# A fp32 decoder trunk on one core: weight combinations of the first FFN tiles on VectorE, and the last operand sets made between the first tile's products

## The chip, the core and the metric

The kernel runs on one core of a Trainium2 chip. A core has TensorE (matmuls, whose sums stand in PSUM), VectorE, ScalarE and GpSimd for work on tiles in SBUF, and SyncE, whose queue issues most of the DMAs. Every engine takes its own instructions in order and waits for the others by semaphores. The metric is the device time of one execution in microseconds; less is better. Names in the profile: PE is TensorE, PEld its weight loads, DVE VectorE, ACT ScalarE, POOL GpSimd, SP SyncE.

## What is computed

The program is a trunk of two layers over 1024 positions of width 1024, in float32. Each layer has a mixer (convolution and gMLP in layer 0, latent attention and mLSTM in layer 1), then a SwiGLU FFN, then a gated embedding. The change lies in the FFN alone, which both layers run:

```python
D_FF = -(-8 * D_MODEL // (3 * 256)) * 256        # 2816

def swiglu(h, w_gate, w_up, w_down):
    return (jax.nn.silu(h @ w_gate) * (h @ w_up)) @ w_down
...
    h = h + swiglu(rmsnorm(h, g_ffn[layer]), w_gate[layer], w_up[layer], w_down[layer])
```

## The kernel before

**Products.** Every fp32 matmul is done as three in a rounded format: each operand x is split into a high part (ScalarE casts it, L146) and a low part x - high (VectorE subtracts, L147), and `mm3` (L189 to L191) issues high x high, high x low and low x high into one PSUM accumulator. A tile is 128 x 512; one split therefore costs one ScalarE and one VectorE instruction.

**The way up.** `h @ w_gate` and `h @ w_up` use a scheme of seven block products in place of eight (Strassen's, in Winograd's form). The activations are cut in four by width and by position, the weights in four by row half and by column half. A unit of work is a pair of output tiles, i and i + 11, for the gate or for the up matrix, so there are 11 gate and 11 up units. Each takes seven products of 12 matmuls, numbered 1 to 7; product k multiplies the k-th combination of weights (made by `w_chain`, L167, and split by `w_halves`) by the k-th set of right operands `XC[k]`, four split tiles (`xch`, `xcl` in the profile). Sets 1 and 2 are made while the mixer ends. Sets 6, 7, 5, 4 and 3 are made by the generator `second_half` of `mixer_out`, in nine steps: four that normalize, subtract and make set 6, two for set 7, and one each for sets 5, 4 and 3. In the profile `h`, `t` are these activations, and L421 and L461 their normalization and subtractions.

**Weights.** `supply` is a second generator, moved on by one step at the end of every product (`prod`). It first loads the weight quarters of products 1 and 2, and then, unit by unit, the four quarters for the rest, forms four combinations of them (L179 to L181 and L510: `sg`, `su` are sums, `rg`, `ru` the loaded quarters of gate and up) and splits them (`hg`, `lg`, `hu`, `lu`). Loaded quarters and combinations share six buffers of tag `raw`. In this version all combinations are made on GpSimd.

**Order of the first units.** `ahead` are the gate and up units of pairs 0 and 1, `third` those of pair 2. Since sets 6 to 3 aren't ready yet, all six units first do products 1 and 2. Product 1's accumulator is copied out (`p1`, L580) and product 2 is then added on top of it in PSUM; the sum of both, after silu for the gate (`out11`, L548) or multiplied by it for the up unit (L551), frees the accumulator. The program holds six such accumulators (`ps`), all taken by these six units. Then `p6` and `rest` do products 6, 7, 5, 4, 3 of each unit in turn: two accumulators `pa`, `pb` are used again for products 4 and 3, after VectorE has read them (L593, L533). For an up unit GpSimd then multiplies by the gate and forms combinations for the way down (L540, L561), which are stored; the next pair's gate writes into the buffers that these stores read. The framework places the instructions of each engine in an order of its own at build time, by dependencies and priorities, so an engine's order isn't that of the code line by line. Where the words "first tile" stand, unit 0 of `ahead` is meant.

Of the kernel before, what the change touches and what calls it, by code (L numbers as in the profile page):

```python
# [16 lines left out]
ALU = mybir.AluOpType  # L17
# [29 lines left out]
class Build:  # L47
# [28 lines left out]
    def name(self, s):  # L76
        self.uid += 1
        return f"{s}_{self.uid}"
# [87 lines left out]
        self.split(hi, lo, t)  # L166
        return [(hi[:, k, :], lo[:, k, :]) for k in range(4)]  # L167

    def w_chain(self, w, c0, c1, name):


        tt = self.nc.gpsimd.tensor_tensor
        raw = lambda: self.wp.tile([P, 4, P], F32, tag="raw", name=self.name(f"s{name}"), bufs=RAW)
        a11 = self.w_quarter(w, 0, c0, name)
        a21 = self.w_quarter(w, 0, c1, name)
        a22 = self.w_quarter(w, 1, c1, name)
        a12 = self.w_quarter(w, 1, c0, name)
        s1, s2 = raw(), raw()
        tt(out=s1, in0=a21, in1=a22, op=ALU.add)  # L179
        tt(out=s2, in0=s1, in1=a11, op=ALU.subtract)  # L180
        tt(out=a21, in0=a11, in1=a21, op=ALU.subtract)  # L181
        return {1: a11, 2: a12, 4: a22, 5: s1, 6: s2, 7: a21}
# [142 lines left out]
def trunk(ctx, tc, x, p, positions, g_mix, g_ffn, g_ple, ev_w_in, ev_w_conv, ev_g_v, ev_w_s,  # L325
          ev_b_s, ev_w_out, od_w_in, od_b_gate, od_g_qa, od_g_kva, od_w_q_up, od_w_kv_up, od_g_q,
          od_g_k, od_g_mh, od_w_out, w_gate, w_up, w_down, w_ple_proj, w_ple_gate, out):
    nc = tc.nc
    B = Build(tc)
    x = x[0]  # L330
    out = out[0]
# [152 lines left out]
    def ffn_up(l, XC, second_half, act_d, down):  # L484

        half = NFF // 2
        sg, act = {}, {}
        c2 = lambda i: slice(i * P, (i + 1) * P)
# [4 lines left out]
        def supply():  # L493


            name = lambda d: "gu"[d["up"]]
            for part in (ahead, third):
                for k in (1, 2):
                    for d in part:
                        t = B.w_quarter(d["w"], k - 1, c2(d["i"]), name(d))  # L500
                        d["u"][k] = B.w_halves(t, name(d))
                        yield
            for d in ahead + third + later:
                i = d["i"]
                r = B.w_chain(d["w"], c2(i), c2(i + half), name(d))
                for k in (6, 7, 5, 4, 3) if i < 3 else (1, 6, 2, 7, 5, 4, 3):
                    d["u"][k] = B.w_halves(r[k], name(d))
                    if k == (6 if i < 3 else 2):
                        r[3] = r[2]
                        nc.gpsimd.tensor_tensor(out=r[3], in0=r[2], in1=r[6], op=ALU.subtract)  # L510
                    yield
            for s in range(AHEAD):
                down(s)
                yield

        def prod(d, k, ps=None):

            begins = ps is None
            ps = B.ps(f"p{k}") if begins else ps
            B.part_mm(ps, d["u"].pop(k), XC[k], begins)  # L520
            next(weights, None)
            return ps

        def spot(d, key):
            j = int(key[0]) * 2 - 3 + int(key[1])
            if not d["up"]:
                return B.slot(56 + d["i"] % 2 * 4 + j, F32, "sg")
            return B.slot(68 if j == 0 and d["i"] % 2 else 64 + j, F32, "act")

        def out(d, key, a, b):  # L530

            t = spot(d, key)
            nc.vector.tensor_tensor(out=t, in0=a, in1=b, op=ALU.add)  # L533
            if not d["up"]:
                nc.scalar.activation(t, t, AF.Silu)
                sg[d["i"], key] = t
                return
            act[d["i"], key] = t
            last = d["i"] == half - 1
            (nc.vector if last else nc.gpsimd).tensor_tensor(  # L540
                out=t, in0=t, in1=sg[d["i"], key], op=ALU.mult
            )
            operands(d["i"], key)

        def out11(d, t):

            if not d["up"]:
                nc.scalar.activation(t, d["X"], AF.Silu)  # L548
                sg[d["i"], "11"] = t
            else:  # L550
                nc.vector.tensor_tensor(out=t, in0=d["X"], in1=sg[d["i"], "11"], op=ALU.mult)  # L551
                act[d["i"], "11"] = t
# [33 lines left out]
            u2 = d["p1"]  # L586
            nc.vector.tensor_tensor(out=u2, in0=prod(d, 6), in1=u2, op=ALU.add)

        def rest(d):
            u2 = d["p1"]  # L590
            pa = prod(d, 7)
            u3 = B.tmp("u3")
            nc.vector.tensor_tensor(out=u3, in0=pa, in1=u2, op=ALU.add)  # L593
            pb = prod(d, 5)
            out(d, "22", pb, u3)
            prod(d, 4, pa)
            out(d, "21", pa, u2)
            prod(d, 3, pb)
            out(d, "12", pb, u2)


        more = second_half()
        ahead = [start(i, up) for i in range(2) for up in range(2)]
        third = [start(2, up) for up in range(2)]
        later = [start(i, up) for i in range(3, half) for up in range(2)]
        early = [dp.tile([P, HT], F32, name=B.name("early")) for _ in range(3)]
# [6 lines left out]
                next(more)  # L613
        for j, d in enumerate(ahead):
            p2(d)
            if j in (1, 2):
                next(more)
        for d, t in zip(third, early):
            p1(d, B.tmp("p1"))
            nc.sync.dma_start(t, d["p1"])  # L620
            next(more)
        for d in third:
            p2(d)
            out11(d, B.tmp("o11"))
            next(more)
        nc.sync.dma_start(early[2], act[2, "11"])
        for _ in more:
            pass
        for d in ahead:
            out11(d, spot(d, "11"))  # L630
        for d in ahead:
            p6(d)
            rest(d)
        for d, t in zip(third, early):
            d["p1"] = load(t, "p1")
            p6(d)
            if d["up"]:
                t = act[2, "11"] = spot(d, "11")
# [9 lines left out]
    half = NFF // 2  # L648
# [304 lines left out]
    for hq in range(2):  # L953
        t = B.tp.tile([P, 4, P], F32, tag="S", name=B.name("wsr"), bufs=2)
        nc.sync.dma_start(t, ev_w_s[0, hq * 4 : hq * 4 + 4].rearrange("h t s -> t h s"))
        nc.gpsimd.affine_select(
            out=t, in_=t, pattern=[[0, 4], [-1, P]], compare_op=ALU.is_ge, fill=0.0, base=0,
# [82 lines left out]
    for ch in range(4):  # L1040
# [13 lines left out]
        for n in range(2):  # L1054
# [6 lines left out]
            w = [col(CONV + i * 4 + ch) for i in range(3)]  # L1061
            nc.scalar.activation(y, z[n][:, 2:], AF.Copy, scale=w[2])
            for i in (1, 0):
                nc.vector.scalar_tensor_tensor(
                    out=y, in0=z[n][:, i : i + HT], scalar=w[i], in1=y, op0=ALU.mult, op1=ALU.add
# [127 lines left out]
    for i in range(16):  # L1193
# [3 lines left out]
        out=ang, in0=posf.unsqueeze(2).to_broadcast([P, NT, 16]),  # L1197
        in1=freq.unsqueeze(1).to_broadcast([P, NT, 16]), op=ALU.mult,
# [3 lines left out]
        out=turns, in0=ang, scalar1=1.0 / (2 * math.pi), scalar2=ROUND, op0=ALU.mult, op1=ALU.add  # L1202
    )
    nc.vector.tensor_scalar(
        out=turns, in0=turns, scalar1=-ROUND, scalar2=None, op0=ALU.add
    )
    fl = lambda t: t.rearrange("p a b -> p (a b)")
    for c in (TWO_PI_A, TWO_PI_B, TWO_PI_C):
        nc.vector.scalar_tensor_tensor(
            out=fl(ang), in0=fl(turns), scalar=-c, in1=fl(ang), op0=ALU.mult, op1=ALU.add  # L1210
        )
    nc.vector.tensor_scalar(
        out=ang, in0=ang, scalar1=3.1415925, scalar2=-3.1415925, op0=ALU.min, op1=ALU.max
# [5 lines left out]
        out=fl(ang), in0=fl(ang), scalar=-1.0, in1=fl(ang), op0=ALU.mult, op1=ALU.max  # L1219
    )  # L1220
    nc.vector.tensor_scalar(
        out=ang, in0=ang, scalar1=-1.0, scalar2=math.pi / 2, op0=ALU.mult, op1=ALU.add
# [10 lines left out]
        out=qsc[0:NOPE, :], in0=vec[0:NOPE, G_Q : G_Q + 1], scalar1=sc, scalar2=None, op0=ALU.mult  # L1233
# [200 lines left out]
    for tt in range(NT):  # L1434
# [3 lines left out]
        for c in range(2):  # L1438
# [6 lines left out]
            out=q[:, :, 0:NOPE], in0=q[:, :, 0:NOPE],  # L1445
            in1=rn.unsqueeze(2).to_broadcast([P, H, NOPE]), op=ALU.mult,
# [386 lines left out]
    ahead = 0  # L1833
# [106 lines left out]
```

## Time and profile before

| what | us |
|---|---|
| median of 3 runs | 2507.98 (2502.91 to 2508.26) |
| the profiled execution's own time | 2521.44 |
| its span | 2519.4 |
| TensorE busy | 2452.2 (97%) |
| VectorE busy | 1563.8 (62%) |
| ScalarE busy | 986.8 (39%) |
| GpSimd busy | 993.0 (39%) |

The profile records one execution. The span goes from its first to its last instruction. Busy time is the sum over the engine's instructions, and idle time is put down to the instruction that had to wait, with what released it. The way up of layer 0 begins at 354.85 us and that of layer 1 at 1729.6 us. PEclk is the clock that TensorE was granted, as a share of 2.4 GHz: 0.50 is 1.2 GHz.

### The profile page before, as it was taken

How to read it: one execution, taken by the hardware profiler on the slowest of the kernel's cores; microseconds unless marked ns; L12 is line 12 of the kernel's file. 1: busy time of each engine (PE TensorE's matmuls, PEld its weight loads, DVE VectorE, ACT ScalarE, POOL GpSimd, SP SyncE). 2: the span in 40 equal slices, each digit the busy share in tenths (PEclk: the TensorE clock that was granted, in tenths of full speed). 3: DMA queues.
4: the chain of work that ended last, by engine and by line, in shares of the span. 5: the costliest groups of instructions: out<-in, count | busy, mean ns of one | idle time of the engine just before them, and what ended most of it. 6: DMA issues, size and time to landing. Idle time of an engine off the chain costs nothing. (4 is left out here: it accounts for less than half of the span.)

```text
span 2519.4 us, 34032 instructions
## 1 busy us (share of the span) xinstructions
PE 2452.2 (97%) x11510; PEld 2025.9 (80%) x11510; DVE 1563.8 (62%) x2879; ACT 986.8 (39%) x1877; POOL 993.0 (39%) x878
## 2 busy tenths in 40 slices
PE   7999998999999999999999999999999999999999
PEld 6878886888888887789888788877788888887877
DVE  6863487544556888776775447548655554697832
ACT  5321343333234545444554345635332332454521
POOL 3451125655642754222221122113566565285400
PEclk9999999999999999999999869999999999999999
DMA  4221543423336767552446633154333333776820
GB/s 147 84 77 49 155 142 108 140 88 105 110 99 236 246 202 257 168 158 82 117 146 177 168 86 104 47 155 134 118 117 112 94 109 100 251 263 195 289 98 38
DMA packets 358687, 350.75 MB, mean 139 GB/s; under 512 B 24012, under 2 KB 249649, under 8 KB 358513
## 3 DMA queue, kind: packets, MB, share of 16 engines
q1 hardware_dynamic: 358016, 348.25, 43.9%
q8 instruction: 90, 1.47, 0.2%
q0 software_dynamic: 464, 0.33, 0.1%
q14 instruction: 85, 0.69, 0.1%
q10 hardware_dynamic: 32, 0.01, 0.0%
HBM read 255.18 MB, written 93.32 MB: 138 GB/s over the span
## 5 line engine op out<-in xcount | busy, mean ns | idle before, releaser
L189 PE MATMUL pd<-acth,hd 128*128 128x512 f32 x616 | 242.3, 393 | 11.5 <-DVE res L723 11.5
L190 PE MATMUL pd<-actl,hd 128*128 128x512 f32 x616 | 241.5, 392 | 0.0
L191 PE MATMUL pd<-acth,ld 128*128 128x512 f32 x616 | 241.4, 392 | 0.0
L259 POOL TENSOR_TENSOR S<-S,sq 128x512 f32<-128x512 f32 x62 | 89.3, 1440 | 257.5 <-ACT sq L257 256.7
L189 PE MATMUL p<-xch,hg 128*128 128x512 f32 x440 | 175.6, 399 | 12.3 <-ACT o L548 10.0
L191 PE MATMUL p<-xch,lg 128*128 128x512 f32 x440 | 174.7, 397 | 0.0
L190 PE MATMUL p<-xcl,hg 128*128 128x512 f32 x440 | 174.4, 396 | 0.0
L191 PE MATMUL p<-xch,lu 128*128 128x512 f32 x440 | 173.0, 393 | 0.0
L189 PE MATMUL p<-xch,hu 128*128 128x512 f32 x440 | 173.0, 393 | 0.0
L190 PE MATMUL p<-xcl,hu 128*128 128x512 f32 x440 | 172.7, 393 | 0.0
L147 DVE TENSOR_TENSOR actl<-ra,acth 128x512 fp32r<-128x512 f32 x154 | 166.3, 1082 | 10.2 <-ACT acth L146 10.1
L189 PEld LDWEIGHTS pd<-acth,hd 128*128 128x128 f32 x616 | 116.8, 190 | 36.7 <-DVE res L723 12.4
L146 ACT CAST hu<-ru 128x512 fp32r<-128x512 f32 x116 | 71.6, 622 | 188.8 <-PE p L190 176.4
L191 PEld LDWEIGHTS pd<-acth,ld 128*128 128x128 f32 x616 | 116.7, 189 | 24.4
L190 PEld LDWEIGHTS pd<-actl,hd 128*128 128x128 f32 x616 | 116.8, 190 | 24.1
L147 DVE TENSOR_TENSOR ld<-rd,hd 128x512 fp32r<-128x512 f32 x110 | 100.8, 916 | 52.8 <-ACT hd L146 52.5
L146 ACT CAST hg<-rg 128x512 fp32r<-128x512 f32 x110 | 68.2, 620 | 158.4 <-PE p L190 132.1
L540 POOL TENSOR_TENSOR act<-act,sg 128x512 f32<-128x512 f32 x60 | 88.5, 1478 | 103.2 <-DVE act L533 103.0
L146 ACT CAST hd<-rd 128x512 fp32r<-128x512 f32 x110 | 68.2, 620 | 143.6 <-PE pd L190 62.7
L147 DVE TENSOR_TENSOR lu<-ru,hu 128x512 fp32r<-128x512 f32 x116 | 114.8, 990 | 15.1 <-ACT hu L146 15.1
L189 PEld LDWEIGHTS p<-xch,hg 128*128 128x128 f32 x440 | 83.9, 191 | 33.6 <-ACT o L548 10.9
L146 ACT CAST acth<-ra 128x512 fp32r<-128x512 f32 x154 | 94.7, 616 | 22.3 <-DMA ra<-act 16.8
(553 smaller groups left out, 6871.2 us busy)
## 6 DMA issues: line engine op xcount, KB each, us to landing
rd<-in_w_down SPq DMA_DIRECT2D x198, 256.0 KB, 3.8
ra<-act SPq DMA_DIRECT2D x154, 256.0 KB, 3.8
rg<-in_w_gate SPq DMA_DIRECT2D x100, 256.0 KB, 3.2
ru<-in_w_up SPq DMA_DIRECT2D x100, 256.0 KB, 2.9
act<-act SPq DMA_DIRECT2D x88, 256.0 KB, 2.0
act<-at SPq DMA_DIRECT2D x66, 256.0 KB, 2.0
rpg<-in_w_ple_gate SPq DMA_DIRECT2D x48, 256.0 KB, 3.0
rwo<-in_ev_w_out SPq DMA_DIRECT2D x32, 256.0 KB, 2.8
```

The costliest lines, as they stand in the source:

```text
L146: self.nc.scalar.copy(hi, src)
L147: (eng or self.nc.vector).tensor_tensor(out=lo, in0=src, in1=hi.bitcast(F32), op=ALU.subtract)
L189: mm(ps, a[0], b[0], start=first, stop=False, skip_group_check=more)
L190: mm(ps, a[0], b[1], start=False, stop=False, skip_group_check=more)
L191: mm(ps, a[1], b[0], start=False, stop=last, skip_group_check=more)
L259: eng.tensor_tensor(out=st[n], in0=st[n], in1=sq, op=ALU.add)
L540: (nc.vector if last else nc.gpsimd).tensor_tensor(out=t, in0=t, in1=sg[d["i"], key], op=ALU.mult)
```

## The change

The combinations of the first three units (gate and up of pair 0, gate of pair 1) go to VectorE: `w_chain` takes the engine as an argument. The steps of `second_half` are spread otherwise: the first five are as early as before or a product or two later, the second step for set 7 comes after the products 2 of `third`, and those for sets 5, 4 and 3 come inside product 6 and `rest` of the first unit. `out11` of the units in `ahead` is issued inside their own `rest`, behind product 7, and no longer for all four ahead of the first product 6.

```diff
--- before.py
+++ after.py
@@ -166,10 +166,10 @@
         self.split(hi, lo, t)
         return [(hi[:, k, :], lo[:, k, :]) for k in range(4)]
 
-    def w_chain(self, w, c0, c1, name):
-
-
-        tt = self.nc.gpsimd.tensor_tensor
+    def w_chain(self, w, c0, c1, name, eng):
+
+
+        tt = eng.tensor_tensor
         raw = lambda: self.wp.tile([P, 4, P], F32, tag="raw", name=self.name(f"s{name}"), bufs=RAW)
         a11 = self.w_quarter(w, 0, c0, name)
         a21 = self.w_quarter(w, 0, c1, name)
@@ -502,12 +502,13 @@
                         yield
             for d in ahead + third + later:
                 i = d["i"]
-                r = B.w_chain(d["w"], c2(i), c2(i + half), name(d))
+                eng = nc.vector if d in ahead[:3] else nc.gpsimd
+                r = B.w_chain(d["w"], c2(i), c2(i + half), name(d), eng)
                 for k in (6, 7, 5, 4, 3) if i < 3 else (1, 6, 2, 7, 5, 4, 3):
                     d["u"][k] = B.w_halves(r[k], name(d))
                     if k == (6 if i < 3 else 2):
                         r[3] = r[2]
-                        nc.gpsimd.tensor_tensor(out=r[3], in0=r[2], in1=r[6], op=ALU.subtract)
+                        eng.tensor_tensor(out=r[3], in0=r[2], in1=r[6], op=ALU.subtract)
                     yield
             for s in range(AHEAD):
                 down(s)
@@ -586,13 +587,17 @@
             u2 = d["p1"]
             nc.vector.tensor_tensor(out=u2, in0=prod(d, 6), in1=u2, op=ALU.add)
 
-        def rest(d):
+        def rest(d, more=iter(())):
             u2 = d["p1"]
             pa = prod(d, 7)
             u3 = B.tmp("u3")
             nc.vector.tensor_tensor(out=u3, in0=pa, in1=u2, op=ALU.add)
+            next(more, None)
+            if "11" in d:
+                out11(d, spot(d, "11"))
             pb = prod(d, 5)
             out(d, "22", pb, u3)
+            next(more, None)
             prod(d, 4, pa)
             out(d, "21", pa, u2)
             prod(d, 3, pb)
@@ -613,24 +618,23 @@
                 next(more)
         for j, d in enumerate(ahead):
             p2(d)
-            if j in (1, 2):
+            if j % 2:
                 next(more)
-        for d, t in zip(third, early):
+        for j, (d, t) in enumerate(zip(third, early)):
             p1(d, B.tmp("p1"))
             nc.sync.dma_start(t, d["p1"])
-            next(more)
+            if j:
+                next(more)
         for d in third:
             p2(d)
             out11(d, B.tmp("o11"))
-            next(more)
+        next(more)
         nc.sync.dma_start(early[2], act[2, "11"])
-        for _ in more:
-            pass
-        for d in ahead:
-            out11(d, spot(d, "11"))
         for d in ahead:
             p6(d)
-            rest(d)
+            next(more, None)
+            d["11"] = True
+            rest(d, more)
         for d, t in zip(third, early):
             d["p1"] = load(t, "p1")
             p6(d)
```

What this does to the order on each engine, in layer 0 (layer 1 has the same):

VectorE, where the first unit's weights are combined; before, these rows hold only the activations (`h`, `t`) and low halves of weights (`lu`, `lg`) and operands (`xcl`):

```order
L421 SCALAR_TENSOR_TENSOR h_2972<-h_2972,vec,R_3303 128x512
L461 TENSOR_TENSOR h_2385<-h_2777,h_2385 128x512
L421 SCALAR_TENSOR_TENSOR h_2822<-h_2822,vec,R_3303 128x512
L461 TENSOR_TENSOR t_807_3367<-h_2972,h_2385 128x512
L147 TENSOR_TENSOR lg_3400<-sg_3395,hg_3399 128x512
L461 TENSOR_TENSOR h_2565<-h_2565,t_807_3367 128x512
L147 TENSOR_TENSOR xcl_3370<-t_807_3367,xch_3369 128x512
L147 TENSOR_TENSOR lg_3417<-rg_3388,hg_3416 128x512
L421 SCALAR_TENSOR_TENSOR h_3022<-h_3022,vec,R_3303 128x512
```

And now, from the same first row:

```order
L421 SCALAR_TENSOR_TENSOR h_2972<-h_2972,vec,R_3303 128x512
L461 TENSOR_TENSOR h_2385<-h_2777,h_2385 128x512
L179 TENSOR_TENSOR sg_3394<-rg_3388,rg_3390 128x512
L461 TENSOR_TENSOR t_807_3367<-h_2972,h_2385 128x512
L180 TENSOR_TENSOR sg_3395<-sg_3394,rg_3386 128x512
L461 TENSOR_TENSOR h_2565<-h_2565,t_807_3367 128x512
L147 TENSOR_TENSOR xcl_3370<-t_807_3367,xch_3369 128x512
L181 TENSOR_TENSOR rg_3388<-rg_3386,rg_3388 128x512
L147 TENSOR_TENSOR lg_3400<-sg_3395,hg_3399 128x512
L511 TENSOR_TENSOR rg_3392<-rg_3392,sg_3395 128x512
L147 TENSOR_TENSOR lg_3417<-rg_3388,hg_3416 128x512
L421 SCALAR_TENSOR_TENSOR h_2822<-h_2822,vec,R_3303 128x512
```

The four combinations (L179, L180, L181, L511) stand between the subtractions; the last two rows of activations shown before come later, behind the low halves of weights.

ScalarE, from the cast ahead of the first copy of `third` (`p_830` is its copy, `p_831` its accumulator) to the first silu, `o`. Before:

```order
L146 CAST xch_3451<-t_825_3449 128x512
L580 COPY p_830_3472<-p_831_3473 128x512
L146 CAST xch_3493<-h_2728 128x512
L146 CAST xch_3610<-h_2655 128x512
L580 COPY p_838_3502<-p_839_3503 128x512
L146 CAST hu_3529<-su_3525 128x512
L146 CAST xch_3498<-h_2777 128x512
L146 CAST xch_3537<-h_2822 128x512
L146 CAST xch_3627<-h_3077 128x512
L146 CAST hu_3558<-ru_3518 128x512
L548 ACT_TABLE_LOAD
L548 ACTIVATE o_854_3562<-p_831_3473 128x512
```

And now:

```order
L146 CAST xch_3613<-h_2475 128x512
L581 COPY p_830_3472<-p_831_3473 128x512
L146 CAST xch_3467<-t_827_3465 128x512
L146 CAST xch_3648<-h_2655 128x512
L581 COPY p_834_3492<-p_835_3493 128x512
L146 CAST hu_3519<-su_3515 128x512
L549 ACT_TABLE_LOAD
L549 ACTIVATE o_850_3552<-p_831_3473 128x512
```

Between the first copy and the silu there were seven casts of operands and weights, with a cast of GpSimd's sum `su` among them; now there are three, and that sum is VectorE's.

VectorE, at the third product of the first up unit (`act_38..` are its results, `lu_38..` the low halves of the fourth unit's weights). Before:

```order
L593 TENSOR_TENSOR u_915_3783<-p_912_3766,p_787_3286 128x512
L147 TENSOR_TENSOR lg_3780<-rg_3695,hg_3779 128x512
L533 TENSOR_TENSOR act_3816<-p_916_3785,u_915_3783 128x512
L147 TENSOR_TENSOR lu_3812<-su_3807,hu_3811 128x512
L533 TENSOR_TENSOR act_3836<-p_912_3766,p_787_3286 128x512
L147 TENSOR_TENSOR lu_3833<-ru_3800,hu_3832 128x512
L533 TENSOR_TENSOR act_3856<-p_916_3785,p_787_3286 128x512
```

And now:

```order
L594 TENSOR_TENSOR u_912_3777<-p_909_3760,p_787_3286 128x512
L552 TENSOR_TENSOR act_3779<-p_788_3287,sg_3652 128x512
L147 TENSOR_TENSOR lu_3808<-su_3803,hu_3807 128x512
L534 TENSOR_TENSOR act_3812<-p_914_3781,u_912_3777 128x512
L552 TENSOR_TENSOR act_4015<-p_803_3344,sg_3904 128x512
L534 TENSOR_TENSOR act_3832<-p_909_3760,p_787_3286 128x512
L147 TENSOR_TENSOR lu_3829<-ru_3796,hu_3828 128x512
L534 TENSOR_TENSOR act_3852<-p_914_3781,p_787_3286 128x512
```

The first low half of the fourth unit stood behind the first result of the up unit; now it stands ahead of it, and two results of `out11` (L552) have come in between.

## Rows read from the trace of the kernel before

**Rows 1.** The page: span and busy time, share of the span, instructions.

```profile
span 2519.4 us, 34032 instructions
...
PE 2452.2 (97%) x11510; PEld 2025.9 (80%) x11510; DVE 1563.8 (62%) x2879; ACT 986.8 (39%) x1877; POOL 993.0 (39%) x878
```

**Rows 2.** TensorE's waits: line, releaser: us in total, times, longest.

```profile
PE p L189 <- ACT o L548: 10.0, 2, 5.7
PE p L189 <- ACT p L580: 5.9, 2, 2.9
```

**Rows 3.** Windows: busy us (instructions) of each engine, PEclk, DMA share, GB/s.

```profile
398.86:403.30 4.44, 4.44 (x11) 3.48 (x12) 4.44 (x9) 1.47 (x3) 0.00 (x0) 0.50 0.22 64
...
1762.16:1765.30 3.14, 3.14 (x8) 2.52 (x9) 3.02 (x6) 1.47 (x3) 3.14 (x1) 0.51 0.22 84
```

**Rows 4.** Order of time, TensorE, layer 0: start, us, line, [idle before].

```profile
384.07 0.39 PE L191 MATMUL p<-xbh,lu 128*128 128x512 f32 x1
387.40 0.50 PE L189 MATMUL p<-xbh,hg 128*128 128x512 f32 x1 [2.94 <-ACT p L580]
...
398.86 0.79 PE L189 MATMUL p<-xch,hg 128*128 128x512 f32 x1 [5.70 <-ACT o L548]
...
403.29 0.40 PE L190 MATMUL p<-xcl,hg 128*128 128x512 f32 x1
...
440.58 0.47 PE L189 MATMUL p<-xch,hg 128*128 128x512 f32 x1 [0.50 <-DVE sg L533]
```

**Rows 5.** The same in layer 1.

```profile
1762.16 0.80 PE L189 MATMUL p<-xbh,hg 128*128 128x512 f32 x1 [2.94 <-ACT p L580]
...
1773.63 0.80 PE L189 MATMUL p<-xch,hg 128*128 128x512 f32 x1 [4.31 <-ACT o L548]
...
1815.90 0.47 PE L189 MATMUL p<-xch,hg 128*128 128x512 f32 x1 [0.82 <-DVE sg L533]
```

**Rows 6.** Order of time, ScalarE, layer 0.

```profile
386.77 0.58 ACT L580 COPY p<-p 128x512 f32<-128x512 f32 x1
...
394.20 0.62 ACT L146 CAST hu<-su 128x512 fp32r<-128x512 f32 x1 [5.32 <-POOL su L180]
...
396.91 1.28 ACT L548 ACT_TABLE_LOAD   x1
398.21 0.60 ACT L548 ACTIVATE o<-p 128x512 f32<-128x512 f32 x1
```

**Rows 7.** Order of time, GpSimd, layer 0.

```profile
385.69 5.88 POOL L179 TENSOR_TENSOR su<-ru,ru 128x512 f32<-128x512 f32 x1 [9.84 <-DVE lg L147]
...
420.71 1.29 POOL L179 TENSOR_TENSOR su<-ru,ru 128x512 f32<-128x512 f32 x1 [5.66 <-DVE lg L147]
...
423.68 1.28 POOL L180 TENSOR_TENSOR su<-su,ru 128x512 f32<-128x512 f32 x1
```

**Rows 8.** Order of time, VectorE, layer 0.

```profile
367.62 1.80 DVE L421 SCALAR_TENSOR_TENSOR h<-h,vec,R 128x512 f32<-128x512 f32 x1
369.34 1.77 DVE L461 TENSOR_TENSOR h<-h,t 128x512 f32<-128x512 f32 x1
...
372.25 0.74 DVE L421 SCALAR_TENSOR_TENSOR h<-h,vec,R 128x512 f32<-128x512 f32 x1
...
394.85 1.21 DVE L147 TENSOR_TENSOR lu<-su,hu 128x512 fp32r<-128x512 f32 x1 [4.42 <-ACT hu L146]
...
402.60 4.89 DVE L147 TENSOR_TENSOR xcl<-h,xch 128x512 fp32r<-128x512 f32 x8
...
425.64 1.24 DVE L147 TENSOR_TENSOR lu<-su,hu 128x512 fp32r<-128x512 f32 x1 [1.42 <-ACT hu L146]
...
429.01 0.69 DVE L533 TENSOR_TENSOR act<-p,p 128x512 f32<-128x512 f32 x1 [0.42 <-PE p L191]
...
439.74 0.69 DVE L533 TENSOR_TENSOR sg<-p,u 128x512 f32<-128x512 f32 x1 [3.41 <-DMA act<-at]
```

**Rows 9.** Transfers from 355 to 440 us: count, KB each, median us to landing.

```profile
rg<-in_w_gate SPq DMA_DIRECT2D x11, 256.0 KB, 2.9
```

## The prediction

> **What bounds the kernel now.** I read the page's busy shares first: TensorE is busy for 2452.2 of 2519.4 us, 97% [rows 1], so every change is worth only what it takes from the remaining 67 us of idle time, or from time at the lower clock. TensorE's own list of waits came next. Two of its three largest entries belong to the start of the way up: 10.0 us in two waits for ScalarE's silu at L548, and 5.9 us in two for the copy at L580 [rows 2], one of each per layer. The windows show what followed: after the long wait the granted clock was 0.50 and 11 recorded matmuls took 4.44 us, and in layer 1 it was 0.51 behind the shorter wait, where 8 took 3.14 us [rows 3]. At full clock a matmul here starts every 0.23 us, so these stretches cost 4.44 - 2.53 = 1.9 us and 3.14 - 1.84 = 1.3 us. The order of time on TensorE gives the places: it had issued its work at 384.30, went on at 387.40, waited again until 398.86, and began the third product of the second pair's gate at 440.58, with 0.50 us of idle time ahead of it [rows 4]. Layer 1 is the same 1374.77 us later (1762.16, 1773.63), but reaches that last point 0.55 us later still, at 1815.90 [rows 5].
>
> Why it waited stands on the other engines. The copy at 386.77 sits on ScalarE behind a cast of what VectorE makes. At 394.20 ScalarE stood 5.32 us for GpSimd's sum, and behind it stood a table load of 1.28 us and the silu at 398.21, which frees the accumulator that product 6 wants [rows 6]. GpSimd's sum took 5.88 us from 385.69, against 1.29 us for the same operation at 420.71, when VectorE was less dense [rows 7]. The two engines hurt each other: VectorE's operations at 367.62 and 369.34 took 1.80 and 1.77 us instead of 0.74 and 0.68, and it stood 4.42 us at 394.85, for the cast that waited for GpSimd [rows 8].
>
> **The change part by part.** I walk VectorE's new order from the last row the change leaves alone, h<-h,vec,R at 372.25 [rows 8].
>
> *Combinations on VectorE.* Three weight tiles of four operations are 12 per layer. The nearest row is a run of eight subtractions of the same shape, 4.89 us, or 0.60 us each [rows 8]: 7.2 us in all. What goes is the time lost to GpSimd: 1.80 - 0.74 and 1.77 - 0.68 before 372.25, the same twice more after it, and the 4.42 us; 8.7 us. VectorE's total is therefore not longer, and 372.25 becomes 370.10.
>
> *First wait.* In the new order 21 rows lie between that row and the subtraction (h_2475) on which the cast ahead of the copy waits. Sixteen at 0.60 and five scaled ones at 0.66 (0.74 less the 0.08 by which such rows overlap) make 12.9 us: it starts at 383.0 and ends at 383.7. Cast (0.62) and copy (0.58) [rows 6] end at 384.9. TensorE is ready at 384.30, so 3.10 us of waiting become 0.6.
>
> *Second wait.* 24 matmuls, one every 0.227 us, end at 390.3. The silu must be done by then: VectorE's second operation of the next combination is 6 rows after 383.0, it ends at 387.3, then cast 0.62, table load 1.28 and silu 0.60 end at 389.8. It is covered, by 0.5 us only. Product 6 starts at 390.3 instead of 398.86: 8.5 us. The stretch at half clock behind the old wait (1.9 us) goes with it.
>
> *What is late next.* (a) Product 7 wants the other accumulator, freed by VectorE's multiplication (o) 17 rows after 383.0, that is at 393.2 and done at 393.9, while TensorE is ready at 393.0: 1.0 us. The last operand of set 7 is 22 rows after 383.0, done at 397.0; TensorE mixes products 7 and 5 around it, and I allow 0.7 us. Sets 5, 4 and 3, 7.2 us of subtractions that stood ahead of product 6's result, now stand between the products that come before their use. (b) The fourth tile of the second pair stays on GpSimd, and its weights are loaded into buffers that VectorE frees 43 rows after 383.0, at 409.6. Landing takes 2.9 us [rows 9], GpSimd's three operations took 4.25 us from 420.71 to the end of the one at 423.68 [rows 7], the cast takes 0.62 and VectorE's low half 1.24 as at 425.64 [rows 8]: 418.7. In the new order that low half stands ahead of the addition that frees the accumulator of the first up tile's third product; before, it stood behind it. Behind the waiting row VectorE holds this addition, and TensorE waits for the addition: released at 419.4 to 419.7. TensorE is ready at 390.3 + 1.7 + 110 matmuls. In the run of before the 168 matmuls from 398.86 to 440.58 took 41.72 us, less 1.9 for the clock and 0.5 of waiting 0.234 us each; 110 of these are 25.7, so it is ready at 417.7. New wait: 1.7 to 2.0 us; bounds 0 (loads in time) and 2 + 4.6 (GpSimd's sum again at 5.88). (c) The second pair's gate must not overwrite the first pair's results before they are stored. The first pair's last addition was at 429.01, the gate's first at 439.74, 10.73 us of products on GpSimd and of storing, and TensorE started 0.84 us after that [rows 4, 8]. Now that last addition falls at 419.5 + 12 x 0.234 + 0.1 = 422.4, so the point comes at 434.0. TensorE is ready at 419.5 + 58 x 0.234 = 433.1: 0.9 us of waiting instead of 0.5.
>
> A rule bears on (b). The rows show GpSimd's sum at 5.88 us from 385.69 while VectorE ran without a pause until 390.43, which is 394.85 less its 4.42 us of idle time [rows 7, 8]. The Trainium skill, "SBUF — State Buffer", section "Who interferes with whom", says that a VectorE operation with two SBUF inputs and a GpSimd operation that reads SBUF exclude each other for a whole instruction. Its words would let GpSimd wait for one VectorE operation, 0.6 us, and the sum would be as worked out; the row says that it can lose to many in succession, and by the row the new wait would have its upper bound.
>
> *Sum.* Layer 0: 440.58 - 434.0 = 6.6 us (8.5 + 1.9 - 1.7 - 1.8 - 0.4, within rounding). Layer 1, by its row at 1815.90, 0.5 more: 7.1. Half clock can return behind the new waits: of two waits of 2.94 us one was followed by it, at 1.3 us; the new ones are shorter, and I take it once. 6.6 + 7.1 - 1.3 = 12.4 us. On SP's queue two stores change places with a neighbouring weight load; I cost that at nothing, since those weights are read at least 18 VectorE rows, 10.8 us, after the load can start, and landing takes 2.9. Bounds per layer: nothing gained if GpSimd is 6.8 us later, 9.2 us if (b) and (c) cost nothing.
>
> The profiled execution took 2521.4 us, so it would take 2509. The runs have a median of 2507.98, 13.5 us lower, with the same program; the same gain there gives 2495.6, and I predict 2496.
>
> **The rivals.**
> 1. *Fuller gain*: neither (b) nor (c) waits, no half clock: 2 x (1.8 + 0.9) + 1.3 = 6.7 us more, 2489. For it: loads can land sooner than 2.9 us when little else moves. Against: VectorE's order puts the low half ahead whatever the load does.
> 2. *The gain is given back to the clock*: each layer gets half clock behind the waits of (a) and (b), 1.3 to 1.9 us each time, and (b) is a microsecond longer: 2 x (2 x 1.6 + 1) = 8.4 us off 13.7, 2503; with one more such wait, 2506. For it: 2.94 us of waiting was enough once. Against: no single new wait is that long.
> 3. *Slower*: GpSimd's fourth combination starves under the denser VectorE. Two of its three operations at 5.88 instead of 1.3 are 9.2 us, in VectorE's and so TensorE's way: 6.8 - 9.2 = -2.4 us per layer, with 2.2 of half clock behind a wait that long -4.6, so 2517. It decides from 6.8 us of delay on. Against: VectorE has only a few rows left before it stands itself, and an idle VectorE let GpSimd through in 1.29 us.
> 4. *No effect*, because the copy or the silu is held by something else on ScalarE: 2508. Against: every row between them in the new order is a cast of something VectorE made earlier.
>
> **How the numbers follow.** Forecast 0.57, with its own range of 2491 to 2501; rival 1 0.16; rival 2 0.15; rival 3 0.08; rival 4 0.04. About 0.2%, 5 us, is what a measurement of this kernel can tell from no change: faster means under 2503, slower over 2513. Forecast and rival 1 are faster, and about half of rival 2: 0.80. The other half and rival 4 make 0.12, and rival 3 makes 0.08. The range takes in rivals 1 and 2 with a few us for the spread of the runs (2502.9 to 2508.3): 2486 to 2508; it leaves out rival 3 and the tails.
>
> **What would show it.** Right: TensorE's wait for the copy falls below 1 us and the one for the silu is gone or under 1 us in each layer, no clock of 0.5 near 398; GpSimd is idle from about 363 to 412; a wait of about 2 us for the addition at L534 near 418, with VectorE standing behind ScalarE's cast just before it; the third product of the second pair's gate near 434 and near 1809. Wrong: GpSimd operations of over 3 us near 413, a wait for the silu of several us, half clock behind the new waits, or a third product of that gate near 440.

## The result, and the profile after

The changed kernel takes 2494.57 us (median of 12 runs, 2488.85 to 2510.84) against 2508.12 for the kernel before (12 runs, 2502.01 to 2518.40): a ratio of 0.9949, with a 95% interval from 0.9926 to 0.9971. The forecast was 2496. The profiled executions differ by 10.60 us (2521.44 and 2510.84).

The page after, as [rows 1]:

```profile
span 2509.1 us, 34030 instructions
PE 2450.3 (98%) x11510; PEld 2022.0 (81%) x11510; DVE 1573.8 (63%) x2903; ACT 988.6 (39%) x1877; POOL 948.1 (38%) x854
```

VectorE has 24 instructions more and GpSimd 24 fewer, 12 per layer. VectorE's busy time grows by 10.0 us here, and not by 24 x 0.60 = 14.4. That alone does not show what GpSimd had cost it, since a second profile of the changed kernel has 1567.9 us.

TensorE's waits on the way up (line, releaser: us in total, times, longest), for [rows 2]. A wait of 0.4 us per layer at L299 is the same in every run and left out of this list and the next:

```profile
PE p L189 <- DVE act L534: 4.0, 2, 2.0
PE p L189 <- DVE sg L534: 2.6, 4, 1.0
PE p L189 <- DVE o L552: 1.3, 2, 0.7
PE p L189 <- ACT p L581: 0.9, 2, 0.5
```

The 10.0 us for the silu are gone, and of the 5.9 us for the copy 0.9 are left. New are 4.0 us for the addition at L534 and 1.3 us for the multiplication at L552. Their places, in order of time on TensorE (start, us, line, [idle before]), layer 0 and then layer 1, for [rows 4, 5]; the first and the last row of each layer are the first and the last matmul of its way up:

```profile
354.84 0.39 PE L189 MATMUL p<-xbh,hg 128*128 128x512 f32 x1
...
384.91 0.50 PE L189 MATMUL p<-xbh,hg 128*128 128x512 f32 x1 [0.46 <-ACT p L581]
...
390.50 0.40 PE L189 MATMUL p<-xch,hg 128*128 128x512 f32 x1
...
394.12 0.47 PE L189 MATMUL p<-xch,hg 128*128 128x512 f32 x1 [0.66 <-DVE o L552]
...
419.54 0.50 PE L189 MATMUL p<-xch,hu 128*128 128x512 f32 x1 [1.99 <-DVE act L534]
...
435.75 0.47 PE L189 MATMUL p<-xch,hg 128*128 128x512 f32 x1 [0.99 <-DVE sg L534]
...
789.83 0.40 PE L191 MATMUL p<-xch,lu 128*128 128x512 f32 x1
...
1726.13 0.39 PE L189 MATMUL p<-xbh,hg 128*128 128x512 f32 x1
...
1790.84 0.50 PE L189 MATMUL p<-xch,hu 128*128 128x512 f32 x1 [1.99 <-DVE act L534]
...
1806.76 0.47 PE L189 MATMUL p<-xch,hg 128*128 128x512 f32 x1 [0.66 <-DVE sg L534]
...
2160.98 0.40 PE L191 MATMUL p<-xch,lu 128*128 128x512 f32 x1
```

Product 6 starts at 390.50, and no wait stands ahead of it. The way up, from the start of its first matmul to the start of its last, takes 434.99 and 434.85 us. Before, it ran from 354.85 to 794.65 and from 1729.61 to 2170.00, 439.80 and 440.39. It gained 4.81 + 5.54 = 10.35 us. This sum over both layers (880.19 before, 869.84 after) is what I compare below, because it leaves out what other stages do.

Behind the new wait the clock fell in both layers. Windows (stretch: length, busy us and instructions of TensorE, its weight loads, VectorE, ScalarE, GpSimd; PEclk, DMA share, GB/s):

```profile
419.54:423.00 3.46, 3.46 (x9) 2.75 (x10) 1.93 (x3) 0.00 (x0) 2.97 (x2) 0.58 0.47 152
...
1790.84:1795.50 4.66, 4.66 (x14) 3.64 (x15) 2.12 (x4) 0.62 (x1) 2.98 (x2) 0.65 0.51 169
```

At 0.23 us each the matmuls would have taken 2.1 and 3.2 us, so 1.4 and 1.4 us went to the clock.

What released the two later waits, VectorE in layer 0:

```profile
417.68 1.22 DVE L147 TENSOR_TENSOR lu<-su,hu 128x512 fp32r<-128x512 f32 x1 [3.27 <-ACT hu L146]
418.81 0.68 DVE L534 TENSOR_TENSOR act<-p,u 128x512 f32<-128x512 f32 x1
...
434.91 0.69 DVE L534 TENSOR_TENSOR sg<-p,u 128x512 f32<-128x512 f32 x1 [3.41 <-DMA act<-at]
```

VectorE stood 3.27 us for the cast of the fourth unit's weights, which GpSimd had made, with the addition that TensorE wanted behind it; and 3.41 us for the store of the first pair's results.

### The profile page after: what moved, and what is told of

Same layout as the page of the kernel before. It is cut to its first block, busy times and chain, and to the rows that moved or that the text cites. A ratio compares the mean times of both kernels' runs of the same rounds, so it can differ in the third digit from the quotient of the medians.

```text
span 2509.1 us, 34030 instructions
## 1 busy us (share of the span) xinstructions
PE 2450.3 (98%) x11510; PEld 2022.0 (81%) x11510; DVE 1573.8 (63%) x2903; ACT 988.6 (39%) x1877; POOL 948.1 (38%) x854
## 4 chain that ended last, share of the span: by engine, by line
PE 80%; DVE 8%; DMA 4%; issue 3%; POOL 3%; ACT 1%; SPq 0%; POOLq 0%; DVEq 0%; ACTq 0%
PE p L189 10%; PE p L190 10%; PE p L191 10%; PE pd L189 5%; PE pd L190 5%; PE pd L191 5%; PE O L1832 3%; PE ppg L190 2%; PE ppg L189 2%; PE ppg L191 2%; PE po L189 2%; PE po L190 2%; PE po L191 2%; PE PT L1874 1%; PE S L1774 1%
## 5 line engine op out<-in xcount | busy, mean ns | idle before, releaser
L147 DVE TENSOR_TENSOR ld<-rd,hd 128x512 fp32r<-128x512 f32 x110 | 106.7, 970 | 51.0 <-ACT hd L146 50.9
```

What stands on the lines that cost most here:

```text
L147: (eng or self.nc.vector).tensor_tensor(out=lo, in0=src, in1=hi.bitcast(F32), op=ALU.subtract)
```

## The experiments

Of each run the way up's sum over both layers is read from its trace, and TensorE's waits there. The times of one kernel spread by 20 us for a reason that lies elsewhere (last section), so the sums tell more than the medians. Two profiles of the changed kernel differ by 1.69 us in this sum, so I read nothing from less than 2 us.

Each ratio is against the runs of before made beside it, four sets with medians of 2506.69 to 2509.14; the first row has one of them.

| kernel | median us (runs) | ratio to before, 95% | way up, two layers, us | against before |
|---|---|---|---|---|
| before | 2507.22 (29) | | 880.19 | |
| changed | 2494.57 (12) | 0.9949 [0.9926, 0.9971] | 869.84 | -10.35 |
| engine alone | 2497.65 (12) | 0.9969 [0.9945, 0.9992] | 870.37 | -9.82 |
| order alone | 2510.98 (12) | 1.0013 [0.9990, 1.0036] | 887.51 | +7.32 |
| four units | 2499.56 (12) | 0.9970 [0.9946, 0.9993] | 876.68 | -3.51 |
| exchange, three units | 2496.55 (9) | 0.9948 [0.9919, 0.9978] | 866.32 | -13.87 |
| exchange, four units | 2480.40 (6) | 0.9884 [0.9854, 0.9914] | 858.44 | -21.75 |
| the same, old order | 2490.43 (11) | 0.9934 [0.9909, 0.9959] | 865.27 | -14.92 |
| exchange, five units | 2484.97 (12) | 0.9919 [0.9893, 0.9945] | 863.35 | -16.84 |
| changed + 4 idle GpSimd additions | 2503.45 (12) | 0.9978 [0.9959, 0.9997] | 877.49 | -2.70 |
| changed, again | 2493.59 (12) | 0.9942 [0.9921, 0.9964] | 868.15 | -12.04 |
| exchange, four units, again | 2492.01 (6) | 0.9917 [0.9890, 0.9945] | 858.43 | -21.76 |

**Engine alone.** The kernel before, its order kept, with `w_chain` taking the engine and in `supply`

```diff
-                r = B.w_chain(d["w"], c2(i), c2(i + half), name(d))
+                eng = nc.vector if d in ahead[:3] else nc.gpsimd
+                r = B.w_chain(d["w"], c2(i), c2(i + half), name(d), eng)
```

> The kernel before, with the combinations of the first three units on VectorE and nothing else changed: sets 5, 4 and 3 and the silus of the first four units stay ahead of the first product 6. Theory A (the gain is from taking the combinations off GpSimd, whose sum of 5.88 us held ScalarE's cast, copy and silu): 2495 to 2500 us against 2508, the wait for the copy under 1 us per layer, no GpSimd operation of over 3 us between 360 and 412 us, and the third product of the second pair's gate within 1 us of the changed kernel's. A wait of 2 to 4 us for the silu may stay, since nothing hides it by order. Rival B (the gain is from the order: the later silus and sets): 2505 to 2509, that third product near 440.

A holds: the median lies in its range, although four of the twelve runs took 2503 to 2509 and one 2513, and the trace agrees. The wait for the copy is gone from the list, and 9.82 of the 10.35 us are there. The second pair's gate starts its third product 81.10 us after the first product, against 80.91 in the changed kernel. GpSimd is idle from 363 to 414. A wait for a silu stayed, 2.96 us in each layer, now that of the second tile's gate (`sg`):

```profile
395.50 0.50 PE L189 MATMUL p<-xch,hg 128*128 128x512 f32 x1 [2.96 <-ACT sg L549]
```

**Order alone.** The changed kernel, with

```diff
-                eng = nc.vector if d in ahead[:3] else nc.gpsimd
+                eng = nc.gpsimd
```

> The changed kernel with all combinations on GpSimd again: the new order alone. Theory A: 2505 to 2512 us; GpSimd's first sums take over 3 us again, TensorE waits about 3 us for the copy and 3 to 6 us for the silu in each layer, third product of the second pair's gate at 440 to 443. Rival B: 2495 to 2499, the wait for the silu gone although GpSimd's sum is slow, since sets 5, 4 and 3 no longer stand ahead of it.

A holds: no gain (the way up is 7.32 us longer, which the times can't tell from before), and the waits are back (2.87 us for the copy, 3.80 for the silu, and 2.15 for an addition). One part of A fell: GpSimd's sums were not slow. At the very place where one took 5.88 us before [rows 7], it took 1.65, and this time VectorE paid. GpSimd and VectorE in this run:

```profile
385.71 1.65 POOL L179 TENSOR_TENSOR su<-ru,ru 128x512 f32<-128x512 f32 x1 [9.28 <-DVE lg L147]
387.44 1.60 POOL L181 TENSOR_TENSOR ru<-ru,ru 128x512 f32<-128x512 f32 x1
```

```profile
385.55 2.36 DVE L461 TENSOR_TENSOR h<-h,h 128x512 f32<-128x512 f32 x2
387.83 1.75 DVE L461 TENSOR_TENSOR t<-h,h 128x512 f32<-128x512 f32 x1
389.51 0.68 DVE L461 TENSOR_TENSOR h<-h,h 128x512 f32<-128x512 f32 x1
```

Beside a GpSimd operation VectorE's takes 1.75 us instead of 0.68. ScalarE's wait for the sum fell from 5.32 us [rows 6] to 1.50, and yet the first silu began 43.03 us after the way up's first matmul, against 43.36 before. The starved sum was thus one form of the cost and not its cause.

**GpSimd beside VectorE, alone.** To see whether VectorE's loss reaches the end without anyone waiting for GpSimd's results, the changed kernel got four additions that nobody reads:

```diff
+                if d is ahead[0]:
+                    for k in range(4):
+                        a, b = XC[1][k], XC[2][k]
+                        nc.gpsimd.tensor_tensor(out=B.slot(57, F32, "idle"), in0=a[0].bitcast(F32), in1=b[0].bitcast(F32), op=ALU.add)
```

> The changed kernel with four more additions on GpSimd, of operands of sets 1 and 2 into a free buffer that nobody reads; they run at about 363 to 370 us, where GpSimd combined the first unit's weights before. Nothing waits for them and VectorE's order is unchanged. Theory A1 (what GpSimd's combinations cost is VectorE's time beside them, 1.1 us for each): four VectorE operations take 1.8 instead of 0.7 us, VectorE reaches the subtraction ahead of the first copy 4.3 us later, the wait for the copy grows from 0.46 to 4 to 5 us in each layer, with half clock behind it: 8 to 13 us slower than the changed kernel, 2503 to 2508. Rival A2 (what they cost is only that ScalarE and VectorE wait for their results): 2493 to 2497, waits as in the changed kernel.

The place was missed: GpSimd stood until 397.6, released by a cast of ScalarE, so the additions ran there and not at 363, and the wait for the copy stayed at 0.44 us. The price was there all the same. GpSimd and VectorE with them:

```profile
397.58 7.87 POOL L509 TENSOR_TENSOR idle<-xbh,xbh 128x512 f32<-128x512 f32 x4 [35.09 <-ACT hu L146]
```

```profile
399.74 6.26 DVE L147 TENSOR_TENSOR xcl<-h,xch 128x512 fp32r<-128x512 f32 x4
```

And VectorE's same four subtractions in the second profile of the changed kernel:

```profile
401.55 2.49 DVE L147 TENSOR_TENSOR xcl<-h,xch 128x512 fp32r<-128x512 f32 x4
```

3.77 us more, 0.94 for each GpSimd operation. TensorE then waited three times 0.72 to 0.74 us for these operands and 2.30 instead of 2.01 us for the addition (four lines were put in, so that L538 here is L534 elsewhere):

```profile
422.53 0.72 PE L189 MATMUL p<-xch,hu 128*128 128x512 f32 x1 [2.30 <-DVE act L538]
```

Counted from its first matmul, the way up comes to this row after 68.48 us, in the second profile of the changed kernel after 64.72: VectorE's 3.77 us arrived whole. The way up grew by 7.65 us against the first profile of the changed kernel, which like this run had half clock behind that wait in both layers, and by 9.34 against the second, which had it in one (868.15); the medians beside it differ by 9.86. So A1 is shown as a mechanism, at another place than expected. The Trainium skill, "SBUF — State Buffer", section "Who interferes with whom", says that a VectorE instruction with two SBUF inputs and a GpSimd one that reads SBUF keep each other out for a whole instruction. The 1.75 and 6.26 us agree with it. Why GpSimd once waited through eight VectorE operations in a row [rows 7, 8] and at the same place in the order-alone run got through at once is not settled.

**Four units.** The changed kernel, with the fourth unit on VectorE too:

```diff
-                eng = nc.vector if d in ahead[:3] else nc.gpsimd
+                eng = nc.vector if d in ahead else nc.gpsimd
```

> The changed kernel with the fourth unit's combinations (up tile of pair 1) on VectorE too. Theory A, part (b): the wait of 1.99 us at the first up unit's third product comes from that unit's low half, late by GpSimd, standing ahead of the addition; without GpSimd it goes, and with it the half clock behind it: 2 x (2.0 + 1.6) = 7.2 us less at most, 2488 to 2492. Rival C: the low half of the next unit on GpSimd, the fifth, takes its place, and TensorE waits as long some products later; 2493 to 2498, no change against the changed kernel.

The wait at L534 for `act` did go, so (b) was what the prediction said. But rival C's mechanism came, and not "as long" but three times as long: TensorE waited 5.89 us for the second pair's gate in each layer, and the median lies 1.6 us over C's range. VectorE and then TensorE there:

```profile
426.59 0.68 DVE L147 TENSOR_TENSOR lu<-ru,hu 128x512 fp32r<-128x512 f32 x1
435.39 1.21 DVE L147 TENSOR_TENSOR lg<-sg,hg 128x512 fp32r<-128x512 f32 x1 [8.12 <-ACT hg L146]
436.52 0.68 DVE L534 TENSOR_TENSOR sg<-p,u 128x512 f32<-128x512 f32 x1
...
437.34 0.77 PE L189 MATMUL p<-xch,hg 128*128 128x512 f32 x1 [5.89 <-DVE sg L534]
```

The low half of the fifth unit, whose sum GpSimd could make only after the first pair's products, stood ahead of the addition. The half clock behind a wait that long made it worse (0.50 over 3.66 us from 437.34).

**The exchange.** In `operands`, the store issued last no longer holds the buffer that the next gate's first result needs:

```diff
-                t1 = minus(spare(1), a0, a1)
+                t1 = minus(spare(3), a0, a1)
...
-                keep(4, minus(spare(3), b1, t2))
+                keep(4, minus(spare(1), b1, t2))
```

With three units, as in the changed kernel:

> The changed kernel with two of the four buffers of the way down's combinations exchanged, so that the next gate's result doesn't wait for the store that is issued last; three units on VectorE as in the changed kernel. If (c) is the store and nothing else: the wait of 0.99 us at the second pair's gate goes, its third product comes about 1 us earlier, 434.7 in layer 0; the wait of 1.99 us for the addition at L534 and the half clock behind it stay; 2 us less than the changed kernel, 2491 to 2495 (not told apart from it by the times, but by the rows). Rival: VectorE's order also changes, because the place of an instruction follows when its operands are expected; then the wait at L534 moves too, and the time can go either way by up to 6 us per layer.

The wait of 0.99 us is gone, and the 1.99 us at L534 stayed (2.03 and 1.96). The way up gained 3.52 us more on the changed kernel's first profile and 1.83 on its second. The median missed the expected range by 1.5 us, as four of the nine runs took 2503 to 2506; the other five took 2484.5 to 2496.6. With four units ("the run before it" is the one with four units alone):

> As the run before it, and two of the four buffers of the way down's combinations exchange their places, so that the next gate's result doesn't wait for the store that is issued last. If the waits for the late low half (b) and for the store (c) are independent and both real: the third product of the second pair's gate near 431 instead of 435.7 in layer 0 and as much earlier in layer 1, 2484 to 2489 us. Rival: whatever is taken from these waits comes back at the next dependence (fifth unit's low half), 2493 to 2498.

Both waits are gone; TensorE's list for the way up is now

```profile
PE p L189 <- DVE o L552: 1.3, 2, 0.7
PE p L189 <- ACT p L581: 0.9, 2, 0.5
```

VectorE shows why the four units pay here and didn't alone:

```profile
427.79 0.69 DVE L534 TENSOR_TENSOR sg<-p,u 128x512 f32<-128x512 f32 x1 [1.56 <-PE p L191]
434.42 1.23 DVE L147 TENSOR_TENSOR lg<-sg,hg 128x512 fp32r<-128x512 f32 x1 [5.95 <-ACT hg L146]
```

The late low half is as late as before, but the addition now stands ahead of it: with the exchange it no longer depends on the last store, and the framework has placed it earlier. One edit alone gains 3.52 us on the changed kernel, the other loses 6.84, both together gain 11.40: the two waits weren't independent. The median came out 3.6 us under the expected range; a second set of runs should tell luck from gain:

> The best version once more (four units on VectorE, the two buffers exchanged): if its 2480 is the way up's 21.8 us and not a lucky set of runs, 2477 to 2489 with some runs near 2500 where the stretch at half clock near 1434 is long; 11 to 14 us less than the changed kernel's fast runs beside it.

The way up is the same to 0.01 us, but the times missed: the median lies 3 us over the range, and only 1.6 us under the changed kernel's beside it (2493.59), where 11 to 14 were expected. The granted clock differed, 0.990 to 0.993 in the first six runs and 0.984 to 0.990 in these. What the clock cost a run can be estimated as its span times one minus its granted clock. Less that, the medians of the two sets are 2460.0 and 2458.2 us, and those of the changed kernel's two sets 2466.3 and 2466.8: 6 to 9 us faster. As they stand, the twelve runs have a median of 2484.2, 9.6 us under the changed kernel's over its 24 (2493.8). The second profile of the changed kernel, run beside it:

> The changed kernel itself once more, beside the run with GpSimd's four additions and the best version so far: 2490 to 2500, as before, with the same waits (0.46, 0.66, 1.99, 0.99 us) to 0.1 us. How far the runs of one kernel differ should follow the length of the stretch at half clock in the mixer of layer 1 near 1434 us: a profile with a mean clock of 0.990 has a short one (14 to 24 us), one of 0.982 a long one (51 to 55).

The waits came out the same within 0.03 us, and with a mean clock of 0.990 the stretch near 1434 was short (granted clock 0.67 and 0.65 in the two windows of 10 us from 1430, 1.00 after). Its way up is 1.69 us shorter, nearly all of it in layer 0 (433.45), where the wait of 2.01 us at 420.60 was not followed by half clock:

```profile
420.60:424.60 4.00, 4.00 (x17) 3.30 (x18) 2.87 (x5) 0.62 (x1) 3.10 (x3) 1.00 0.42 135
```

**Old order, four units, exchange.** The engine-alone kernel with four units and the exchange:

```diff
-                eng = nc.vector if d in ahead[:3] else nc.gpsimd
+                eng = nc.vector if d in ahead else nc.gpsimd
...
-                t1 = minus(spare(1), a0, a1)
+                t1 = minus(spare(3), a0, a1)
...
-                keep(4, minus(spare(3), b1, t2))
+                keep(4, minus(spare(1), b1, t2))
```

> The best version so far (four units on VectorE, the two buffers exchanged) with the steps of the sets and the silus in the order of the kernel before. If the order matters once VectorE makes the combinations: TensorE waits about 3 us for the silu of the second tile's gate near 395 as in the run with the engine change alone, with half clock behind it, 1.6 us: up to 9 us over both layers, 2484 to 2490. If the order is worth nothing by itself: 2478 to 2483, as the best version so far.

The order matters here: TensorE waits 2.95 us for the silu in each layer, at granted clocks of 0.51 and 0.63 behind it, and the way up is 6.83 us longer than in the new order. In layer 0:

```profile
395.82 0.79 PE L189 MATMUL p<-xch,hg 128*128 128x512 f32 x1 [2.95 <-ACT sg L549]
```

The median, 0.4 us over the expected range, has four runs of 2499 to 2503.

**Five units, exchange.** As the exchange with four units, and

```diff
-                eng = nc.vector if d in ahead else nc.gpsimd
+                eng = nc.vector if d in ahead + third[:1] else nc.gpsimd
```

> The best version so far with the fifth unit's combinations (gate of pair 2) on VectorE too, so that its low half no longer stands behind GpSimd's products of the first pair, as at 434.42 after 5.95 us. That wait is VectorE's and TensorE doesn't wait for it there: if so, 2478 to 2484, no gain. Rival: it holds something later that the waits do not show; 2472 to 2477. Against it: four more operations on VectorE between the products can hold an addition back: up to 2488.

The way up is 4.91 us longer than with four: TensorE waits 0.83 us for an addition at L594 and 1.14 us for one at L534, in layer 1 as long to 0.05 us. In layer 0:

```profile
429.75 0.47 PE L189 MATMUL p<-xch,hg 128*128 128x512 f32 x1 [0.83 <-DVE u L594]
...
433.87 0.47 PE L189 MATMUL p<-xch,hg 128*128 128x512 f32 x1 [1.14 <-DVE sg L534]
```

VectorE's combinations run there beside GpSimd's products of the first pair and take up to 1.67 us. So what stood against the rival came true. The time tells less: the median is 1 us over the range for no gain, and the ratio, 0.9919, is outside the interval of the best version's first set and inside that of its second.

## Why the prediction was right

Point by point, layer 0 unless said otherwise. Rows of the changed kernel for it, from VectorE, ScalarE and GpSimd:

```profile
383.04 0.68 DVE L461 TENSOR_TENSOR h<-h,h 128x512 f32<-128x512 f32 x1
...
389.29 0.60 ACT L549 ACTIVATE o<-p 128x512 f32<-128x512 f32 x1
...
412.57 1.80 POOL L179 TENSOR_TENSOR su<-ru,ru 128x512 f32<-128x512 f32 x1 [49.30 <-DMA ru<-in_w_up]
...
417.02 0.62 ACT L146 CAST hu<-su 128x512 fp32r<-128x512 f32 x1 [4.47 <-POOL su L180]
```

- *Combinations on VectorE.* The subtraction `h_2475` was expected at 383.0 and started at 383.04: 7.2 us of work paid with 8.7 us regained. Two costs went: VectorE slowed beside GpSimd (1.75 us for 0.68), and GpSimd starved once (5.88). Order alone has the waits without the second, and the idle additions show that the first reaches TensorE by itself, though at another place than the first copy.
- *First wait.* 0.6 us expected from 384.30 on, and the product started at 384.91; the profile counts 0.46 us of it as idle. *Second wait.* The silu was to end at 389.8 and product 6 to start at 390.3; they came at 389.89 and 390.50, so the cover was 0.6 us and not 0.5.
- *(a)* Expected 1.0 us, measured 0.66. The 0.7 us allowed for the mixing of products 7 and 5 were not needed; no wait for those operands is in the list.
- *(b)* Expected 1.7 to 2.0 us with a release at 419.4 to 419.7: 1.99 at 419.54. The links on the way agree too: GpSimd was to start at 412.5, and the cast and the low half were to end at 417.4 and 418.7; they came at 412.57, 417.64 and 418.90. Four units removed the wait, as its cause demands.
- *(c)* Expected 0.9 us, measured 0.99; the exchange removed it. From the first pair's last addition (424.19) to the gate's first (434.91) it took 10.72 us, where 10.73 were expected.
- *The clock.* This is the term that was mis-sized: 1.3 us, taken once. In the first profile it came in both layers behind (b), 1.4 us each, and in the second in one. That the new waits are shorter than 2.94 us was no reason against it, and half clock behind them stood among the signs of being wrong. With it the third product of the second pair's gate came at 435.75 and not 434.0; in the second profile 79.35 us after the first product, which is 434.2 on the first profile's time.
- *Sum.* 12.4 us expected; 10.35 and 12.04 in the two profiles of the way up, and 13.5 between the medians. That the median came within 1.4 us of the forecast is in part luck: the interval of the ratio alone is 11 us wide. In layer 1 the third product came at 1806.76, not near 1809, because that way up began 3.48 us earlier; its own gain to this point is 9.14 - 3.48 = 5.7 us, and 7.1 were expected. The 1809 was a slip: it took layer 1's own 7.1 us off and left out that layer 0's gain would move all of layer 1.

Of the rivals, the fuller gain is what the exchange with four units made real: 11.40 us of way up, where 6.7 was estimated for waits and clock. The waits that went make 3.5 us of the 5.7 in layer 0 (those of 1.99, 0.99 and, at the third pair, 0.47) and the clock 1.4; the other 0.8 are not assigned. The gain given back to the clock came in half: behind (b), and not behind (a). The slower case was real as a mechanism: the idle additions took 7.65 to 9.34 us of the gain, though through VectorE's operands and not through a late fourth unit. Its counter-argument was misread: VectorE was not idle beside the sum of 1.29 us at 420.71, it ran an addition out of PSUM at 420.74 and a low half from 421.35, which took 1.21 us. No effect is refuted by the waits.

What the prediction did not see is how the gain divides. The engine alone brings 9.82 of 10.35 us, the order alone costs 7.32. With the engine changed, the order swaps waits: 2.96 us for a silu go, the wait at the second pair's gate falls from 1.59 to 0.99, and the 0.46, 0.66 and 1.99 us of the list above come. The order earns its place only where VectorE makes the combinations and nothing else holds the products: 0.53 us for the change as made, which is less than two profiles of one kernel differ, and 6.83 with four units and the exchange.

## What to carry to other kernels

An engine's operation that runs beside another's can cost the other more than doing the work itself: price a move between VectorE and GpSimd by both engines' rows, 0.60 us for taking it over against 0.9 to 1.1 us for suffering it. Before a late row is removed, look at which row is late next on the same in-order engine, and whether a needed one stands behind it; here one edit lost 6.84 us alone and gained 7.88 after another. Where runs of one kernel spread by more than the change, compare the stage in the trace and not the medians, and more than one profile of it: here two of the same kernel differ by 1.69 us in the stage.

## What the runs showed of the hardware

**One stretch at half clock makes most of the spread.** In the mixer of layer 1, TensorE's clock falls between 1425 and 1445 us in every profile, in a stretch of 10 us in which it was busy for 7.5 to 9.0 us, and stays down for a time that differs between runs of the same kernel. The best version, first and second profile, from 1430 us on (the last three numbers are PEclk, DMA share, GB/s):

```profile
1430.00:1440.00 10.00, 10.00 (x45) 9.64 (x45) 1.92 (x6) 4.55 (x13) 0.61 (x1) 0.50 0.05 13
1440.00:1450.00 10.00, 10.00 (x45) 8.18 (x44) 4.94 (x19) 2.08 (x5) 0.72 (x2) 0.54 0.00 0
1450.00:1460.00 10.00, 9.63 (x72) 7.97 (x72) 6.20 (x20) 5.57 (x18) 5.28 (x11) 1.00 0.64 183
```

```profile
1430.00:1440.00 10.00, 10.00 (x44) 9.06 (x43) 3.20 (x9) 4.28 (x13) 1.35 (x3) 0.50 0.05 15
...
1460.00:1470.00 10.00, 10.00 (x40) 8.27 (x40) 2.27 (x5) 4.00 (x13) 2.65 (x8) 0.50 0.58 155
1470.00:1480.00 10.00, 10.00 (x42) 8.87 (x42) 2.48 (x7) 2.67 (x9) 0.84 (x2) 0.53 0.05 13
```

The stretch is 23.9 us long in the first and 51.2 in the second. Some 27 us more at half clock are 13.5 us of lost work, and the spans differ by 15.2 (2480.5 and 2495.7); another 1.7 us went to half clock from 1390 to 1394, in the second profile alone. In the two profiles of the changed kernel it is 51.2 and 13.7 us long, with spans of 2509.1 and 2491.1 us. The times of all runs agree: the 24 of the changed kernel spread over 24 us, and over 8 us when each is lessened by what its granted clock cost, estimated as for the best version. What ends the stretch in one run earlier than in another, the rows do not show.

**Half clock behind a wait is not certain.** Of four waits of 1.97 to 2.01 us at the same instruction, in two profiles of the changed kernel, three were followed by it; of the waits of 0.3 to 1.6 us on the ways up of all the runs none was, by the clock over the 4 us behind each.
